# A hybrid decoder trunk: weight sums and low parts formed by adding DMAs

## The chip, the core and the metric

The kernel runs on one core of a Trainium2 chip. The metric is the device time in microseconds of one execution. Five engines work side by side, each through its own queue in order: TensorE (matmuls), VectorE, ScalarE, GpSimd and SyncE (SP), which here only issues DMAs. A DMA that adds to what its destination holds is issued by GpSimd (`G.dma_start(..., accum_op=ADD)`).

## The reference

Two layers of a decoder trunk on 512 tokens of width 1024. Each layer does four things, each after an RMSNorm and added to the residual x:

```python
x = x + 0.5 * swiglu_ffn(h, ffn1_w_gate[l], ffn1_w_up[l], ffn1_w_down[l])   # (silu(h Wg) * (h Wu)) Wd, 2816 wide
z = h @ w_in[l]                                  # S5 group (384) | pooling group (256) | conv group (2 x 384)
x = x + concat(S5(z), pool(z), conv(z)) @ w_out[l]
x = x + cross_attention(h, m, wq, wk, wv, wo)    # 4 heads into 256 memory tokens, m = RMSNorm(mem)
x = x + 0.5 * swiglu_ffn(h, ffn2_w_gate[l], ffn2_w_up[l], ffn2_w_down[l])
```

and a final RMSNorm. Everything is float32.

## The kernel before

All float32 products are made of three matmuls on a split into a high part (rounded to the type fp32r) and a low part (the value minus its high part): high x high, high x low, low x high (`mm3`, lines 307 to 309). So every weight that is loaded passes through a split: ScalarE copies it to the high part, and VectorE, or GpSimd where `eng` is G, subtracts to get the low part (`wload`, lines 294 to 301). Raw weights, high parts and low parts have three buffers each (tags raw, wh and wl of the pool wp).

The first feed-forward (ffn1 of layer 0) is a plain one. The other three (ffn2 of layer 0, ffn1 and ffn2 of layer 1) are "seven-product" feed-forwards (`ffn7`): gate and up are computed together by seven half-size products in place of eight, on combinations of the tokens' halves and of the weights' quarters. The hidden width of 2816 is cut into units of 512 columns (five of them, and one of 256). A unit has four weight quarters of two tiles each, (0,0) and (1,0) from the gate, (0,1) and (1,1) from the up matrix. Three steps make sums of weights from them, until now on VectorE:

- `mix1` (line 478): t1 = quarter (0,0) + quarter (0,1), four tiles of 128x512, kept in four buffers of a pool of their own;
- `mix2` (line 482): quarter (0,1) += quarter (1,1), then quarter (0,0) += the new (0,1), two instructions of 128x1024 each;
- `mix3` (line 482): quarter (1,0) += the new (0,0), two more.

The unit's products follow in the order 1 (raw (0,0)), 2 (raw (1,0)), 5 (t1), 6 (mixed (0,0)), 3 (raw (1,1)), 7 (mixed (0,1)), then the down projection of the unit before, then 4 (mixed (1,0)). A product's weights are split two steps ahead of it. In the first unit of a feed-forward t1 and the first sum are formed on GpSimd while the phase before ends (`PairNorm.take`, lines 221 and 223), and the second sum and `mix3` by `sum_` on VectorE.

The mixer runs the input projections, the S5 scan (on TensorE, VectorE, ScalarE and GpSimd in turn), the pooling and a 31-tap convolution on VectorE (line 1053), and fills TensorE meanwhile with the cross-attention's keys and values of the 256 memory tokens (`cross_kv`): eight key tiles of 512 KB (four heads, two halves `dh` of a head) and eight value tiles of 512 KB. The low parts of all of these are subtracted by GpSimd (line 300), which also does the scan's products (lines 992, 1002, 1020) and the norms' powers (line 191). VectorE's steps of the scan are lines 991 to 1003, 1016 and 1022.

The order of each engine's instructions is written out ahead of the run by the framework's planner: it simulates the engines with its own cost model and issues, by priority (the program's order, with the scan and the convolution's end raised), what is ready in that simulation.

Of the kernel before, what the change touches and what calls it, by code (L numbers as in the profile page):

```python
# [9 lines left out]
F32 = mybir.dt.float32  # L10
F32R = mybir.dt.float32r
AF = mybir.ActivationFunctionType
# [5 lines left out]
P = 128  # L18
# [26 lines left out]
def trunk_kernel(ctx: ExitStack, tc: tile.TileContext, io, out, phases=None):  # L45
    nc = tc.nc
    V, A, G, T = nc.vector, nc.scalar, nc.gpsimd, nc.tensor
    ADD, SUB, MUL = ALU.add, ALU.subtract, ALU.mult
# [5 lines left out]
    NK = D // P  # L54
# [35 lines left out]
    def vt(name, shape=(P, 512), dt=F32):  # L90
        return vp.tile(list(shape), dt, tag="V", name=name)
# [10 lines left out]
    def ct_(name, shape, dt=F32):  # L102
        return cp.tile(list(shape), dt, tag="C", name=name)

    def mm(name, shape=(P, 512)):
        return mmp.tile(list(shape), F32, tag="mm", name=name)
# [97 lines left out]
    HK = NK // 2  # L204
# [86 lines left out]
        return rb  # L291


    def wload(src, shape, name, eng=None):
        raw = wp.tile(list(shape), F32, tag="raw", name=f"wr_{name}")
        nc.sync.dma_start(out=raw, in_=src)
        h = wp.tile(list(shape), F32R, tag="wh", name=f"wh_{name}")
        A.activation(out=h, in_=raw, func=AF.Copy)  # L298
        lo = wp.tile(list(shape), F32R, tag="wl", name=f"wl_{name}")
        (eng or V).tensor_tensor(out=lo, in0=raw, in1=h.bitcast(F32), op=SUB)  # L300
        return h, lo

    def wcols(w, r0, nk, c0, name, eng=None):
        return wload(w[r0:r0 + nk * P, c0:c0 + P].rearrange("(k p) c -> p k c", p=P), (P, nk, P), name, eng)

    def mm3(ps, wh, wl, ah, al, first, last, skip=False):
        T.matmul(ps, lhsT=wh, rhs=ah, start=first, stop=False, skip_group_check=skip)  # L307
        T.matmul(ps, lhsT=wh, rhs=al, start=False, stop=False, skip_group_check=skip)  # L308
        T.matmul(ps, lhsT=wl, rhs=ah, start=False, stop=last, skip_group_check=skip)  # L309
# [25 lines left out]
    def rows_pass(dst, w, k0, acts, dh, name, first, last, eng=None, marks=None):  # L335

        n = len(acts)
        got = []
        for j in range(0, n, 2):
            m = min(2, n - j)  # L340
            h, lo = wload(w[(k0 + j) * P:(k0 + j + m) * P, dsl(dh)].rearrange("(k p) c -> p k c", p=P), (P, m, H2),
                          f"{name}_{dh}{j}", eng)
            got += [(h[:, i, :], lo[:, i, :]) for i in range(m)]
            with tc.issue_after(marks[j // 2]) if marks else nullcontext():
                for t, ps in dst:
                    for i in range(m):
                        ah, al = acts[j + i]
                        mm3(ps, ah[:, tsl(t)], al[:, tsl(t)], got[j + i][0], got[j + i][1], first and j + i == 0,
                            last and j + i == n - 1)
        return got  # L350
# [81 lines left out]
    def ffn7(which, l, norm, nxt):  # L432


        wg, wu, wd = (io[f"{which}_w_{n}"][l] for n in ("gate", "up", "down"))
# [27 lines left out]
        class Unit:  # L463
# [10 lines left out]
            def mix1(self):  # L474
                a, b = self.raw[0, 0], self.raw[0, 1]
                t1 = self.raw["t1"] = [vt(f"wt_{self.nm}{k}", (P, self.W)) for k in range(HK)]
                for k in range(HK):
                    V.tensor_tensor(out=t1[k], in0=a[k // 2][:, k % 2, :], in1=b[k // 2][:, k % 2, :], op=ADD)

            def sum_(self, to, other):  # L480
                for a, b in zip(self.raw[to], self.raw[other]):
                    V.tensor_tensor(out=a, in0=b, in1=a, op=ADD)  # L482

            def mix2(self):
                self.sum_((0, 1), (1, 1))
# [77 lines left out]
        for u, un in enumerate(us):  # L563
            b = len(steps)
# [314 lines left out]
    def mixer(l, norm, nxt):  # L879
# [87 lines left out]
        conv_in(2)  # L967

        kv = cross_kv(l, mg)


# [150 lines left out]
    def cross_kv(l, mg):  # L1122
        wk, wv = io["xattn_wk"][l], io["xattn_wv"][l]
        ks, vs = [], []
        for hd in range(NH):
            ps = mm(f"kps{l}_{hd}", (P, 2, M))
            for dh in range(2):
                c0 = hd * HD + dh * P
                h, lo = wcols(wk, 0, NK, c0, f"k{l}_{hd}{dh}", G)
                for k in range(NK):  # L1130
                    mm3(ps[:, dh, :], h[:, k, :], lo[:, k, :], mg[k][:, 0, :], mg[k][:, 1, :], k == 0, k == NK - 1)
            kt = ct_(f"kT{l}_{hd}", (P, 2, 2, M), F32R)
            A.activation(out=kt[:, 0], in_=ps, func=AF.Copy)
            V.tensor_tensor(out=kt[:, 1], in0=ps, in1=kt[:, 0].bitcast(F32), op=SUB)
            ks.append(kt)
        vs = [[ct_(f"v{'hl'[z]}{l}_{m}", (P, D), F32R) for z in range(2)] for m in range(NM)]
        for hf in range(2):
            pss = [mm(f"vps{l}_{hf}{m}") for m in range(NM)]
            for q in range(4):
                h, lo = wload(wv[q * 2 * P:(q + 1) * 2 * P, hf * 512:(hf + 1) * 512].rearrange("(k p) c -> p k c", p=P),  # L1140
                              (P, 2, 512), f"v{l}_{hf}{q}", G)
                for kk in range(2):
                    k = q * 2 + kk
                    for m in range(NM):
                        mh = mg[k][:, 0, m * P:(m + 1) * P]
                        ml = mg[k][:, 1, m * P:(m + 1) * P]
                        T.matmul(pss[m], lhsT=mh, rhs=h[:, kk, :], start=k == 0, stop=False)
                        T.matmul(pss[m], lhsT=mh, rhs=lo[:, kk, :], start=False, stop=False)
                        T.matmul(pss[m], lhsT=ml, rhs=h[:, kk, :], start=False, stop=k == NK - 1)
            for m in range(NM):  # L1150
                sl = slice(hf * 512, (hf + 1) * 512)
                A.activation(out=vs[m][0][:, sl], in_=pss[m], func=AF.Copy)
                V.tensor_tensor(out=vs[m][1][:, sl], in0=pss[m], in1=vs[m][0][:, sl].bitcast(F32), op=SUB)
        return ks, vs
# [222 lines left out]
```

## Time and profile before

| | |
|---|---|
| median of 3 runs | 2134.53 us (2134.12 to 2137.26) |
| profiled execution, its own time | 2135.13 us |
| its span | 2133.0 us |
| mean granted TensorE clock | 0.987 |
| TensorE busy | 2065.5 us (97%) |
| VectorE busy | 1551.3 us (73%) |
| ScalarE busy | 917.0 us (43%) |
| GpSimd busy | 356.8 us (17%) |
| DMA | 229.92 MB, mean 108 GB/s |

The span runs from the first to the last instruction of one execution. Matmuls overlap each other, so that a row's duration of 0.39 us is more than the distance between two starts. The granted clock is what TensorE was given, as a share of full speed. A row of a timeline has its start, its duration, engine, line, operation, output and inputs, shapes and count; in square brackets stands the idle time of the engine before it and what ended that. POOL is GpSimd, PE TensorE, DVE VectorE, ACT ScalarE.

### The profile page before, as it was taken

How to read it: one execution, taken by the hardware profiler on the slowest of the kernel's cores; microseconds unless marked ns; L12 is line 12 of the kernel's file. 1: busy time of each engine (PE TensorE's matmuls, PEld its weight loads, DVE VectorE, ACT ScalarE, POOL GpSimd, SP SyncE). 2: the span in 40 equal slices, each digit the busy share in tenths (PEclk: the TensorE clock that was granted, in tenths of full speed). 3: DMA queues.
4: the chain of work that ended last, by engine and by line, in shares of the span. 5: the costliest groups of instructions: out<-in, count | busy, mean ns of one | idle time of the engine just before them, and what ended most of it. 6: DMA issues, size and time to landing. Idle time of an engine off the chain costs nothing.

```text
span 2133.0 us, 27561 instructions
## 1 busy us (share of the span) xinstructions
PE 2065.5 (97%) x10228; PEld 1732.9 (81%) x10228; DVE 1551.3 (73%) x2574; ACT 917.0 (43%) x1528; POOL 356.8 (17%) x349
## 2 busy tenths in 40 slices
PE   7999999999999999999999999999999999999998
PEld 6778788888788878888878888888877887888886
DVE  5755677579855788787688877666996458887765
ACT  4423333334534464454445444444344345554443
POOL 0377000155400200000110000013661020000000
PEclk9999999998999999999999999999999999999999
DMA  5332445343421323332314223263443232332222
GB/s 170 101 104 82 117 150 165 108 137 107 125 88 60 119 80 119 119 119 79 119 40 147 83 88 108 80 217 97 122 134 109 70 134 79 119 107 91 74 60 84
DMA packets 226750, 229.92 MB, mean 108 GB/s; under 512 B 38478, under 2 KB 152888, under 8 KB 226616
## 3 DMA queue, kind: packets, MB, share of 16 engines
q1 hardware_dynamic: 225952, 227.10, 34.3%
q8 instruction: 80, 1.31, 0.3%
q10 hardware_dynamic: 664, 1.07, 0.1%
q14 instruction: 54, 0.44, 0.1%
HBM read 213.77 MB, written 12.58 MB: 106 GB/s over the span
## 4 chain that ended last, share of the span: by engine, by line
PE 83%; DVE 8%; DMA 3%; ACT 3%; issue 2%; POOL 1%; SPq 1%; DVEq 0%; POOLq 0%; ACTq 0%
PE pxffn L308 6%; PE pxffn L309 6%; PE pxffn L307 6%; PE pddffn L308 5%; PE pddffn L309 5%; PE pddffn L307 5%; PE pzffn L307 3%; PE pzffn L308 3%; PE pzffn L309 3%; PE pdffn L309 2%; PE pdffn L307 2%; PE pdffn L308 2%; DVE cacc L1053 1%; PE qps L308 1%; PE qps L309 1%
## 5 line engine op out<-in xcount | busy, mean ns | idle before, releaser
L308 PE MATMUL pddffn<-wl_dffn,hhffn 128*128 128x512 f32 x480 | 188.9, 394 | 0.0
L309 PE MATMUL pddffn<-wh_dffn,hlffn 128*128 128x512 f32 x480 | 188.1, 392 | 0.0
L307 PE MATMUL pddffn<-wh_dffn,hhffn 128*128 128x512 f32 x480 | 185.8, 391 | 0.0
L1053 DVE SCALAR_TENSOR_TENSOR cacc<-ch,convw,cacc 128x510 f32<-128x510 f32 (+28 forms) x174 | 127.8, 735 | 6.2 <-ACT cacc L1051 2.5
L374 DVE SCALAR_TENSOR_TENSOR x<-pddffn,x 128x512 f32<-128x512 f32 x120 | 82.2, 686 | 62.8 <-PE pddffn L309 62.8
L308 PEld LDWEIGHTS pddffn<-wl_dffn,hhffn 128*128 128x128 f32 x480 | 90.2, 188 | 18.2
L309 PEld LDWEIGHTS pddffn<-wh_dffn,hlffn 128*128 128x128 f32 x480 | 90.2, 188 | 18.0
L307 PEld LDWEIGHTS pddffn<-wh_dffn,hhffn 128*128 128x128 f32 x480 | 89.8, 188 | 18.3
L221 POOL TENSOR_TENSOR wt_first_ffn<-wr_first_ffn,wr_first_ffn 128x512 f32<-128x512 f32 x12 | 16.8, 1426 | 503.3 <-DMA wr_first_ffn<-in_ffn_w_up_dram 503.3
L482 DVE TENSOR_TENSOR wr_ffn<-wr_ffn,wr_ffn 128x1024 f32<-128x1024 f32 (+1 forms) x90 | 98.4, 1110 | 0.1
L300 POOL TENSOR_TENSOR wl_pl<-wr_pl,wh_pl 128x1024 fp32r<-128x1024 f32 x4 | 9.6, 2404 | 486.0 <-ACT wh_pl L298 486.0
L459 DVE TENSOR_TENSOR wl_dffn<-wr_dffn,wh_dffn 128x512 fp32r<-128x512 f32 x60 | 42.0, 705 | 39.7 <-PE pxffn L308 18.2
L535 ACT ACTIVATE hhffn<-htffn 128x512 fp32r<-128x512 f32 x60 | 35.6, 594 | 80.7 <-PE htffn L529 80.6
L307 PE MATMUL pgffn<-xh_ffn,wh_gffn 128*128 128x512 f32 x168 | 66.2, 394 | 0.0
L308 PE MATMUL pgffn<-xl_ffn,wh_gffn 128*128 128x512 f32 x168 | 66.0, 393 | 0.0
L309 PE MATMUL pgffn<-xh_ffn,wl_gffn 128*128 128x512 f32 x168 | 65.9, 392 | 0.0
L309 PE MATMUL puffn<-xh_ffn,wl_uffn 128*128 128x512 f32 x168 | 65.8, 392 | 0.0
L307 PE MATMUL puffn<-xh_ffn,wh_uffn 128*128 128x512 f32 x168 | 65.8, 392 | 0.0
L308 PE MATMUL puffn<-xl_ffn,wh_uffn 128*128 128x512 f32 x168 | 65.8, 392 | 0.0
L191 POOL TENSOR_TENSOR ss_final<-ss_final,nhalf 128x1 f32<-128x1 f32 x4 | 2.2, 550 | 350.2 <-DVE ss_final L190 350.2
L307 PE MATMUL pdffn<-wh_dffn,h_ffffn 128*128 128x512 f32 x144 | 57.9, 402 | 2.1 <-DVE sffn L394 2.1
L300 POOL TENSOR_TENSOR wl_v<-wr_v,wh_v 128x1024 fp32r<-128x1024 f32 x22 | 53.5, 2441 | 35.4 <-ACT wh_v L298 25.7
(745 smaller groups left out, 6735.7 us busy)
## 6 DMA issues: line engine op xcount, KB each, us to landing
wr_dffn<-in_ffn_w_down_dram SPq DMA_DIRECT2D x78, 512.0 KB
wr_ffn<-in_ffn_w_up_dram SPq DMA_DIRECT2D x48, 512.0 KB
wr_ffn<-in_ffn_w_gate_dram SPq DMA_DIRECT2D x48, 512.0 KB
wr_gffn<-in_ffn_w_gate_dram SPq DMA_DIRECT2D x21, 512.0 KB
wr_uffn<-in_ffn_w_up_dram SPq DMA_DIRECT2D x21, 512.0 KB
wr_k<-in_xattn_wk_dram SPq DMA_DIRECT2D x16, 512.0 KB
wr_v<-in_xattn_wv_dram SPq DMA_DIRECT2D x16, 512.0 KB
wr_q<-in_xattn_wq_dram SPq DMA_DIRECT2D x16, 512.0 KB
```

The costliest lines, as they stand in the source:

```text
L191: G.tensor_tensor(out=ss[:, 3:4], in0=ss[:, 2:3], in1=nhalf[:, 0:1], op=ALU.pow)
L221: G.tensor_tensor(out=t1[k], in0=a[k // 2][:, k % 2, :], in1=b[k // 2][:, k % 2, :], op=ADD)
L300: (eng or V).tensor_tensor(out=lo, in0=raw, in1=h.bitcast(F32), op=SUB)
L307: T.matmul(ps, lhsT=wh, rhs=ah, start=first, stop=False, skip_group_check=skip)
L308: T.matmul(ps, lhsT=wh, rhs=al, start=False, stop=False, skip_group_check=skip)
L309: T.matmul(ps, lhsT=wl, rhs=ah, start=False, stop=last, skip_group_check=skip)
L374: V.scalar_tensor_tensor(out=x_, in0=ps, scalar=scale, in1=x_, op0=MUL, op1=ADD)
L459: V.tensor_tensor(out=lo, in0=r, in1=h.bitcast(F32), op=SUB)
L482: V.tensor_tensor(out=a, in0=b, in1=a, op=ADD)
L535: A.activation(out=h, in_=pt, func=AF.Copy)
L1053: V.scalar_tensor_tensor(out=acc[:, d:], in0=h[:, 0:S - d], scalar=cw[:, TAPS - 1 - d:TAPS - d], in1=acc[:, d:], op0=MUL, op1=ADD)
```

## The change

The t1 sums of the units after the first are no longer computed from the loaded quarters: the gate's part is loaded a second time into t1 by SP, and the up matrix' part is added to it from HBM by an adding DMA. The in-place sums of all units become adding DMAs from SBUF to SBUF. In the mixers the low part of all value tiles, and of the key tiles with `dh` = 1, is made in two steps: ScalarE writes the negated high part (a rounded copy with scale -1), and an adding DMA adds the raw weight, from HBM for the values and from the raw tile for the keys. The subtractions of VectorE and GpSimd that did this go.

```diff
+    ADDING = "adding DMA"
+
     def wload(src, shape, name, eng=None):
         raw = wp.tile(list(shape), F32, tag="raw", name=f"wr_{name}")
         nc.sync.dma_start(out=raw, in_=src)
         h = wp.tile(list(shape), F32R, tag="wh", name=f"wh_{name}")
         A.activation(out=h, in_=raw, func=AF.Copy)
         lo = wp.tile(list(shape), F32R, tag="wl", name=f"wl_{name}")
-        (eng or V).tensor_tensor(out=lo, in0=raw, in1=h.bitcast(F32), op=SUB)
+        if eng is ADDING:
+
+            A.activation(out=lo, in_=raw, func=AF.Copy, scale=-1.0)
+            G.dma_start(out=lo, in_=raw if shape[1] > 2 else src, accum_op=ADD)
+        else:
+            (eng or V).tensor_tensor(out=lo, in0=raw, in1=h.bitcast(F32), op=SUB)
         return h, lo
...
                 for k in range(HK):
-                    V.tensor_tensor(out=t1[k], in0=a[k // 2][:, k % 2, :], in1=b[k // 2][:, k % 2, :], op=ADD)
+                    r0 = k * P
+                    nc.sync.dma_start(out=t1[k], in_=wg[r0:r0 + P, self.f0 * P:self.f0 * P + self.W])
+                for k in range(HK):
+                    r0 = k * P
+                    G.dma_start(out=t1[k], in_=wu[r0:r0 + P, self.f0 * P:self.f0 * P + self.W], accum_op=ADD)
 
             def sum_(self, to, other):
                 for a, b in zip(self.raw[to], self.raw[other]):
-                    V.tensor_tensor(out=a, in0=b, in1=a, op=ADD)
+                    G.dma_start(out=a, in_=b, accum_op=ADD)
...
-                h, lo = wcols(wk, 0, NK, c0, f"k{l}_{hd}{dh}", G)
+                h, lo = wcols(wk, 0, NK, c0, f"k{l}_{hd}{dh}", ADDING if dh else G)
...
-                              (P, 2, 512), f"v{l}_{hf}{q}", G)
+                              (P, 2, 512), f"v{l}_{hf}{q}", ADDING)
```

## Rows read from the trace of the kernel before

**Rows 1.** The page's busy times: share of the span, instructions.

```profile
PE 2065.5 (97%) x10228; PEld 1732.9 (81%) x10228; DVE 1551.3 (73%) x2574; ACT 917.0 (43%) x1528; POOL 356.8 (17%) x349
```

**Rows 2.** Busy time by stretch: engines, granted clock, DMA share, GB/s.

```profile
853.00:914.00 61.00, 61.00 (x278) 50.46 (x277) 45.54 (x62) 27.98 (x42) 0.00 (x0) 1.00 0.34 104
...
485.00:570.00 85.00, 80.33 (x444) 69.07 (x443) 80.05 (x111) 37.27 (x50) 49.96 (x24) 0.90 0.38 115
1518.00:1610.00 92.00, 84.97 (x499) 72.42 (x499) 83.71 (x124) 41.51 (x56) 57.27 (x27) 0.96 0.39 119
...
503.00:510.00 7.00, 7.00 (x35) 7.00 (x35) 6.93 (x12) 2.81 (x4) 4.42 (x4) 0.52 0.63 186
524.00:534.00 10.00, 10.00 (x42) 8.97 (x42) 9.15 (x13) 3.57 (x6) 3.58 (x2) 0.50 0.34 116
...
752.00:756.00 4.00, 3.43 (x10) 2.42 (x11) 4.00 (x7) 3.96 (x9) 0.00 (x0) 0.57 0.00 0
```

**Rows 3.** TensorE's waits: who for whom, us in total, times, longest.

```profile
PE yps L1007 <- DVE sy L1003: 5.9, 3, 3.1
PE pxffn L307 <- ACT xc_ffn L258: 5.5, 8, 1.3
...
PE xp_ffn L256 <- DVE xc_ffn L259: 3.9, 3, 1.4
PE gps L1032 <- DVE sys L1022: 3.2, 1, 3.2
...
PE yps L1006 <- DVE sy L991: 1.5, 1, 1.5
```

**Rows 4.** Groups by line: count, busy us, mean ns, idle before.

```profile
L482 DVE TENSOR_TENSOR wr_ffn<-wr_ffn,wr_ffn 128x1024 f32<-128x1024 f32 (+1 forms) x90 | 98.4, 1110 | 0.1
...
L300 POOL TENSOR_TENSOR wl_v<-wr_v,wh_v 128x1024 fp32r<-128x1024 f32 x22 | 53.5, 2441 | 35.4 <-ACT wh_v L298 25.7 <-PE kps L309 6.1 <-issue 3.0
...
L300 POOL TENSOR_TENSOR wl_k<-wr_k,wh_k 128x1024 fp32r<-128x1024 f32 x16 | 40.9, 2560 | 16.5 <-ACT wh_k L298 15.8 <-DVE sy L993 0.8
...
L478 DVE TENSOR_TENSOR wt_ffn<-wr_ffn,wr_ffn 128x512 f32<-128x512 f32 (+1 forms) x60 | 36.0, 634 | 9.4 <-DMA wr_ffn<-in_ffn_w_up_dram 9.3
```

**Rows 5.** Timelines of SP, VectorE and ScalarE before the unit at 910 us.

```profile
882.60 1.57 SPq L656 DMA_DIRECT2D wr_ffn<-in_ffn_w_up_dram  x2
...
896.83 2.35 DVE L482 TENSOR_TENSOR wr_ffn<-wr_ffn,wr_ffn 128x1024 f32<-128x1024 f32 x2
...
919.98 1.06 ACT L448 ACTIVATE wh_ffn_3p<-wr_ffn 128x1024 fp32r<-128x1024 f32 x1 [2.96 <-PE pyffn L309]
```

**Rows 6.** The page's DMA queue; two loads of 512 KB on the chain.

```profile
q1 hardware_dynamic: 225952, 227.10, 34.3%
...
700.22 4.21 DMA wr_xo<-in_xattn_wo_dram
...
1041.40 5.28 DMA wr_dffn<-in_ffn_w_down_dram
```

**Rows 7.** Timelines of VectorE and GpSimd at the second feed-forward's start.

```profile
738.10 1.21 DVE L482 TENSOR_TENSOR wr_first_ffn<-wr_first_ffn,wr_first_ffn 128x1024 f32<-128x1024 f32 x1
...
732.26 0.55 POOL L191 TENSOR_TENSOR ss_ffn<-ss_ffn,nhalf 128x1 f32<-128x1 f32 x1 [5.06 <-DVE ss_ffn L190]
741.31 1.46 POOL L191 TENSOR_TENSOR ss_ffn<-ss_ffn,nhalf 128x1 f32<-128x1 f32 x1 [8.49 <-DVE ss_ffn L190]
```

**Rows 8.** Timeline of VectorE: one scan step beside a subtraction, and alone.

```profile
474.94 2.86 DVE L993 TENSOR_TENSOR sy<-sy,ssw 128x512 f32<-128x512 f32 x1 [0.63 <-POOL ssw L992]
...
509.10 0.68 DVE L993 TENSOR_TENSOR sy<-sy,ssw 128x512 f32<-128x512 f32 x1
```

**Rows 9.** A value tile's copy; the value matmuls' first and last start, both mixers.

```profile
544.33 1.06 ACT L298 ACTIVATE wh_v<-wr_v 128x1024 fp32r<-128x1024 f32 x1 [1.65 <-PE vps L1149]
...
L1147 PE MATMUL vps<-wh_v,mg x32: 387/389/792, 538.6 to 564.1; 128*128 128x512 f32 x32
...
L1147 PE MATMUL vps<-wh_v,mg x32: 387/389/396, 1569.8 to 1597.9; 128*128 128x512 f32 x32
```

## The prediction

> **What bounds the kernel now.** I read the busy times first [rows 1]: TensorE is busy 97% of the span, VectorE 73%, GpSimd 17%. So work taken from VectorE or GpSimd is worth only what TensorE waits for. Then the busy time by stretch [rows 2]. In the steady part of a seven-product feed-forward, here 853 to 914 us, TensorE is busy for all 61.0 us at full clock, although VectorE works 45.5 us of them. In the two mixers' key and value stage it is not: 80.3 of 85 us in the first and 85.0 of 92 in the second, with VectorE at 80.1 and 83.7. Inside the first lie two stretches with the clock granted at its lower level, 1.2 instead of 2.4 GHz: 503 to 510 at 0.52 and 524 to 534 us at 0.50, which cost 3.4 + 5.0 = 8.4 us. The start of the second feed-forward has 4 us at 0.57, worth 1.7. Last, what TensorE waits for [rows 3]: in the mixers VectorE's steps of the S5 scan, 5.9 + 3.2 + 1.5 = 10.6 us; at the starts of the three seven-product feed-forwards evacuations of transposes, 5.5 + 3.9 = 9.4 us, about 3.1 each. What this change can win lies in these waits and the low clock behind them: about 19 us in the mixers and 4 to 5 at a feed-forward's start.
>
> **The feed-forwards' steady part.** VectorE loses the t1 sums and the in-place sums [rows 4]: 60 x 0.634 (36.0 us), 90 x 1.110 (98.4 us) and 12 more of the first units at about 1.1 (13 us), some 148 us. TensorE never waited there, so I count it at nothing. In exchange come, per full unit, four loads of 256 KB on SP's queue, four accumulates of 256 KB from HBM and six of 512 KB inside SBUF on GpSimd's queue, which is otherwise empty in these stretches. What hides them is the lead time [rows 5]: for the unit after the steady one the last up-weights are asked for at 882.6 to 884.2 us, land some 5 us later (5.28 for a load of this size [rows 6]), and the second pair of in-place sums ends at 899.2; the first product that reads it is split on ScalarE at 919.98. An accumulate's whole time, call it D, enters twice in that chain: 889 + D + 1 for the first pair, and the same again for the second. With D = 6 that is 903, with D = 14 it is 919: cover is gone only above about 14 us. The four t1 accumulates stand ahead in GpSimd's queue, but their loads wait only for tiles that the last unit gave back. Term: 0; if the cover fails, each of some 15 units pays the excess.
>
> The transfers' sum bounds this from the other side. The one queue moved 227.1 MB in 34.3% of 2133 us [rows 6], so 512 KB cost the 16 engines 1.69 us; the steady unit has a DMA share of 0.34, 20.7 us [rows 2]. Added: 1.05 MB of loads, 3.4 us, and 4.19 MB of accumulates, 13.5 us if they cost one pass, 40.6 us if three (two reads and a write, one after the other). The sum is 38 to 65 us of 61. I take two passes, 51 us: it fits.
>
> **The feed-forwards' starts.** In the two that follow attention the first unit's sums stand between the last tokens' residual and their normalisation [rows 7]: one of 1.21 us at 738.10, ahead of the mean square in VectorE's order, the other right after it, and beside that one GpSimd's power takes 1.46 us instead of 0.55. Gone, the chain is 1.2 + 0.9 = 2.1 us shorter; TensorE waits about 3.1 us behind it. I take 2.0 each, bounds +1 (an accumulate's issue stands before the power on GpSimd) and -4.8 (all waits and the low clock); the third start, after a feed-forward, had no sum in this place. Term: -4.
>
> **The mixers, GpSimd's side.** GpSimd's subtractions of 2.44 (values, 22 rows of which 16 are these) and 2.56 us (keys, 16) [rows 4] hold up VectorE: the same step of the scan takes 0.68 us alone and 2.86 beside one [rows 8]. I count 18 VectorE instructions stretched like this in the two stages, against the shortest of their kind: 17.6 us beside the keys' subtractions and 5.2 beside the values'. All the values' and half the keys' go: 5.2 + 8.8 = 14.0 us less on a VectorE that is busy 94% and 91% of these stretches, in the chain TensorE waits for. I let half of the 10.6 us of waits go, 5.3, and 3.7 of the 8.4 us of low clock. Term: -9; bounds 0 (the order fixed in TensorE's queue meets another late operand) and -19 (all of both).
>
> **The mixers, the low part's way.** It was ScalarE's copy, then GpSimd's 2.4 us; now two copies of 1.06 us [rows 9] and an accumulate, whose D no row of this trace shows. The nearest rows are loads of 512 KB: 4.21 and 5.28 us [rows 6]. One pass more for reading the destination gives 4.21 + 1.69 = 5.9, two passes 5.28 + 3.4 = 8.7; from below it is 4.2. I take 6. Each weight tile has three buffers, and in the value stage ScalarE's copy waits for TensorE to give one back [rows 9]. A tile's cycle is then two copies, D, and 12 matmuls at 61.0/278 = 0.219 us each [rows 2], 2.63; a third of it is one tile's pace: (2.12 + 6 + 2.63)/3 = 3.58 us. Eight tiles took 25.5 and 28.1 us to the start of the last three matmuls, 0.7 more to their end [rows 9]: 3.27 and 3.60 each. Lost: 8 x 0.31 + 0 = 2.5 us. Half the keys alternate with the old way, and their matmuls lie among the scan's, so D hides there. What queues behind a waiting accumulate is the scan's products on GpSimd, which stood behind waiting subtractions before; ScalarE gets 24 x 1.06 = 25 us more, in stretches in which it is busy 37 of 85 us. Term: +3; bounds 0 (D up to 5.0) and +17 (D = 8.7).
>
> The Trainium skill's DMA: Bandwidth & Descriptors (Anatomy of one DMA — SWDGE (gpsimd) path) fits a DMA issued by GpSimd as 2.0 us plus bytes at 436 GB/s, 3.2 us for 512 KB; by that estimate, which no run here shows and which is not said of accumulates, the last term is 0 and the time 2122.
>
> **Sum.** 0 - 4 - 9 + 3 = -10 us on the profiled execution's 2135.1 (span 2133.0): 2125.1. That execution stands 0.6 above the median of 2134.5, so 2125 stays.
>
> **Rivals.**
> 1. The waits vanish whole: with the scan on time no low clock follows, the value stage keeps its pace and the starts give 3 each: -6 - 14 = 2115, to a few us less. For it: the low stretches follow waits. Against it: VectorE stays busy with the convolutions.
> 2. The issue itself meets VectorE. GpSimd's power of 0.55 us took 1.46 beside a two-input sum [rows 7]; if each accumulate's issue waits like that for one such instruction of 1.2 us, D is 7.2, a tile's pace (2.12 + 7.2 + 2.63)/3 = 3.98, lost 8 x (7.97 - 6.87) = 8.8, and -13 + 8.8 = -4.2: 2131, no change. It is no change too where the saved VectorE time only moves slack. The Trainium skill's same page (SWDGE vs HWDGE vs iDMA) says that GpSimd writes its descriptors to rings in SBUF and that VectorE can lock it out meanwhile; the power's row agrees in kind, no row shows an issue.
> 3. Slower: the value stage becomes a ring of three late low parts. It decides from D = 8.8: pace 4.52, lost 8 x (9.03 - 6.87) = 17.3, more than the 13 won by 4.3 (0.2%). At D = 10 the pace is 4.92, lost 23.7: 2146. For it: 8.7 is one end of my bounds, and the values' source is HBM. Against it: TensorE has scan and gate matmuls to put between.
> 4. The DMA engines are full in the feed-forwards: at three passes 65 us of transfers per 61 us unit, 4 x 15 = 60 us less the 13 won: up to 2182. Against: the lead time, and that the last units are half as wide.
>
> **Chances.** Forecast (2121 to 2130) 0.42, rival 1 0.13, rival 2 0.20, rival 3 0.17, rival 4 0.08. A measurement of this kernel tells about 0.2% (4.3 us) from no change. Faster 0.55, within 0.2% 0.20, slower 0.25. The likeliest case's own range is 2121 to 2130; the range for 8 in 10 is 2114 to 2149, which leaves out rival 4 and the far end of rival 1.
>
> **What would show it.** VectorE's busy time down by about 160 us, GpSimd's by about 60 less what issues cost, TensorE's matmul count the same. The stretched scan steps back at 0.7 us beside the values; TensorE's waits for the scan below 6 us; the power at the two starts back at 0.55. The value stage's 25.5 and 28.1: up by 3 in sum is my D, up by 10 or more in sum is rival 3. No wait of TensorE or ScalarE on an accumulate in the steady feed-forward; any there is rival 4's side and makes the forecast wrong, as would scan waits as long as now.

## The result, and the profile after

The changed kernel takes 2172.84 us (median of 4 runs, 2170.38 to 2175.34) against 2134.36 (4 runs) for the kernel before: ratio 1.0174, 95% interval 1.0158 to 1.0189. It is slower by 38.5 us; 2125 was forecast, and 2149 was the upper end of the range.

From the first start of one phase's transposes on TensorE to the next one's, the first mixer went from 195.5 to 214.5 us and the second from 191.8 to 207.8: +19.0 and +16.0. All other phases together changed by +3.6, the start before them by 0.3. So the place is the mixers, and there the value stage. Page of the changed kernel: busy times, the two queues that carry nearly all bytes (packets, MB, share of 16 engines), and the group of the values' accumulates on GpSimd (busy, mean ns, idle before):

```profile
PE 2077.8 (96%) x10228; PEld 1739.9 (80%) x10228; DVE 1405.2 (65%) x2412; ACT 944.0 (43%) x1552; POOL 457.5 (21%) x511
...
q1 hardware_dynamic: 234592, 241.26, 35.4%
q0 software_dynamic: 28832, 75.51, 19.2%
...
L305 POOL DMA_DIRECT2D wl_v<-in_xattn_wv_dram x16 | 19.5, 1220 | 83.6 <-issue 43.9 <-ACT wh_v L300 14.9 <-ACT su L1046 10.6
```

Against [rows 1] VectorE has lost 146 us (160 were forecast), and GpSimd, whose busy time now holds the issues, has gained 101. The last row is the trace of what went wrong: before 16 issues GpSimd sat idle 83.6 us, over half of it for "issue", which is a wait for nothing that the profile shows. What TensorE waits for in the changed kernel (us, times, longest):

```profile
PE vps L1159 <- DMA wl_v<-in_xattn_wv_dram: 35.1, 12, 5.5
...
PE pxffn L314 <- ACT xc_ffn L258: 4.2, 6, 1.4
PE kps L316 <- DMA wl_k<-wr_k: 3.4, 2, 2.9
PE xp_ffn L256 <- DVE xc_ffn L259: 3.2, 3, 1.2
...
PE yps L1018 <- DVE sy L1014: 1.8, 2, 1.4
```

Beside [rows 3] the scan's waits of 10.6 us are down to 1.8, but a new wait of 35.1 us for the values' low parts has come. The value matmuls of the changed kernel, first to last start, in both mixers:

```profile
L1158 PE MATMUL vps<-wh_v,mg x32: 387/393/632, 530.2 to 584.0; 128*128 128x512 f32 x32
...
L1158 PE MATMUL vps<-wh_v,mg x32: 388/389/796, 1583.7 to 1634.5; 128*128 128x512 f32 x32
```

The changed kernel's busy time in these stretches and in the steady feed-forward, columns as in [rows 2]:

```profile
530.20:584.00 53.80, 35.62 (x107) 24.69 (x106) 26.39 (x34) 21.16 (x25) 14.66 (x10) 0.81 0.74 165
1583.70:1634.50 50.80, 33.77 (x111) 22.49 (x110) 29.71 (x35) 21.13 (x25) 14.54 (x10) 0.90 0.76 164
...
851.00:912.00 61.00, 61.00 (x278) 50.49 (x277) 38.26 (x54) 27.88 (x41) 8.79 (x10) 1.00 0.73 188
```

Eight value tiles take 53.8 and 50.8 us where they took 25.5 and 28.1 [rows 9]. TensorE works 66% of that time, and its clock is granted at 0.81 and 0.90. The steady feed-forward is as full as before: 61.0 of 61.0 us, with the DMA share up from 0.34 to 0.73.

GpSimd's timeline in the first value stage of the changed kernel says what the low parts wait for (start, duration; idle time before in brackets):

```profile
523.66 1.25 POOL L305 DMA_DIRECT2D wl_v<-in_xattn_wv_dram  x1 [1.92 <-ACT wl_v L304]
530.65 1.23 POOL L305 DMA_DIRECT2D wl_v<-in_xattn_wv_dram  x1 [5.74 <-PE kps L316]
538.37 1.21 POOL L305 DMA_DIRECT2D wl_v<-in_xattn_wv_dram  x1 [6.49 <-issue]
547.01 1.21 POOL L305 DMA_DIRECT2D wl_v<-in_xattn_wv_dram  x1 [7.43 <-issue]
...
560.59 1.23 POOL L305 DMA_DIRECT2D wl_v<-in_xattn_wv_dram  x1 [5.92 <-issue]
```

ScalarE's timeline there has two of the negated copies:

```profile
532.99 1.99 ACT L304 ACTIVATE wl_v<-wr_v 128x1024 fp32r<-128x1024 f32 x2
```

They were ready at 534 and 535 us; their accumulates were issued at 538.37 and 547.01. All issues lie 6.5 to 9.6 us apart, and the median from issue to landing is 6.4. The chain of the changed kernel has two of these accumulates, from issue to landing:

```profile
530.65 7.38 DMA wl_v<-in_xattn_wv_dram
...
553.47 6.80 DMA wl_v<-in_xattn_wv_dram
```

They land at 538.03 and 560.27, and the next ones are issued at 538.37 and 560.59. In both mixers each of the 14 issues that follow another comes 0.32 to 0.34 us after the landing of the one before: one value accumulate is on its way at a time. Landing times in the changed kernel (KB each, median us):

```profile
wr_ffn<-wr_ffn POOLq DMA_DIRECT2D x72, 512.0 KB, 4.8
...
wt_ffn<-in_ffn_w_up_dram POOLq DMA_DIRECT2D x48, 256.0 KB, 5.8
...
wl_v<-in_xattn_wv_dram POOLq DMA_DIRECT2D x16, 512.0 KB, 6.4
```

GpSimd's timeline of the changed kernel in a feed-forward, with the issues of four t1 sums:

```profile
876.24 2.69 POOL L489 DMA_DIRECT2D wt_ffn<-in_ffn_w_up_dram  x3 [7.75 <-DMA wt_ffn<-in_ffn_w_gate_dram]
881.17 0.86 POOL L489 DMA_DIRECT2D wt_ffn<-in_ffn_w_up_dram  x1 [2.24 <-DVE wl_ffn_2p L466]
```

Three t1 sums go out within 2.7 us, the fourth about 5 us after the first, when that one has landed; in 14 of the 15 units the fourth comes 0.3 us after that landing. The difference is in the pieces. A t1 sum or a key tile has one piece per partition; a value tile from HBM has two. The packets of this queue show it. In the run with the values alone (below) it carries their 16 accumulates, 272 packets each:

```profile
q0 software_dynamic: 4352, 8.39, 2.5%
```

In the run with the keys alone it carries eight of the same size, 144 packets each:

```profile
q0 software_dynamic: 1152, 4.19, 1.0%
```

My theory from here: GpSimd's descriptors lie in a ring of limited memory (`dynamic_dma_scratch_size=1024` where the kernel is built) that holds three DMAs of 128 pieces and only one of 256, and the next issue waits for it to empty.

### The profile page after: what moved, and what is told of

It is laid out like the page before. It is cut to its first block, busy times and chain, and to the rows that moved or that the text cites. A ratio compares the mean times of both kernels' runs of the same rounds, so it can differ in the third digit from the quotient of the medians.

```text
span 2171.9 us, 28147 instructions
## 1 busy us (share of the span) xinstructions
PE 2077.8 (96%) x10228; PEld 1739.9 (80%) x10228; DVE 1405.2 (65%) x2412; ACT 944.0 (43%) x1552; POOL 457.5 (21%) x511
## 4 chain that ended last, share of the span: by engine, by line
PE 83%; DVE 6%; issue 4%; DMA 3%; ACT 2%; POOL 1%; SPq 0%; POOLq 0%; DVEq 0%; ACTq 0%
PE pxffn L316 5%; PE pxffn L315 5%; PE pxffn L314 5%; PE pddffn L315 5%; PE pddffn L316 5%; PE pddffn L314 5%; PE pzffn L314 3%; PE pzffn L315 3%; PE pzffn L316 3%; PE pgffn L315 2%; PE pgffn L314 2%; PE pgffn L316 2%; PE puffn L316 2%; PE puffn L314 2%; PE puffn L315 2%
## 5 line engine op out<-in xcount | busy, mean ns | idle before, releaser
L493 POOL DMA_DIRECT2D wr_ffn<-wr_ffn x90 | 78.5, 887 | 583.6 <-DVE x L381 241.7
L489 POOL DMA_DIRECT2D wt_ffn<-in_ffn_w_up_dram x60 | 53.2, 1025 | 154.8 <-DMA wt_ffn<-in_ffn_w_gate_dram 76.5
L546 ACT ACTIVATE hhffn<-htffn 128x512 fp32r<-128x512 f32 x60 | 35.8, 596 | 105.7 <-PE htffn L540 105.7
L466 DVE TENSOR_TENSOR wl_dffn<-wr_dffn,wh_dffn 128x512 fp32r<-128x512 f32 x60 | 41.2, 686 | 45.4 <-PE pxffn L315 21.5
L1159 PE MATMUL vps<-wl_v,mg 128*128 128x512 f32 x64 | 31.9, 498 | 35.2 <-DMA wl_v<-in_xattn_wv_dram 35.1
L547 DVE TENSOR_TENSOR hlffn<-htffn,hhffn 128x512 fp32r<-128x512 f32 x60 | 41.2, 687 | 32.7 <-ACT hhffn L546 32.7
L315 PE MATMUL qps<-xl_att,wh_q 128*128 128x256 f32 (+1 forms) x176 | 60.9, 346 | 0.0
```

Of the source, the lines that this page charges most:

```text
L466: V.tensor_tensor(out=lo, in0=r, in1=h.bitcast(F32), op=SUB)
L489: G.dma_start(out=t1[k], in_=wu[r0:r0 + P, self.f0 * P:self.f0 * P + self.W], accum_op=ADD)
L493: G.dma_start(out=a, in_=b, accum_op=ADD)
L546: A.activation(out=h, in_=pt, func=AF.Copy)
L547: V.tensor_tensor(out=lo, in0=pt, in1=h.bitcast(F32), op=SUB)
```

## Experiments

Each kernel is compared with the kernel before on the same chip. The first four tell the values from the rest, and the ring from the three weight buffers.

**The values alone.** The kernel before, with only this of the change:

```diff
-                              (P, 2, 512), f"v{l}_{hf}{q}", G)
+                              (P, 2, 512), f"v{l}_{hf}{q}", ADDING)
```

> The kernel before with only the value tiles' low parts by adding DMAs. Theory (the value stage alone): 2165 to 2178, value stage 50 to 55 us in each mixer, issues of the values' DMAs 6 to 9 us apart. Rival (it takes the feed-forwards' traffic or the keys' DMAs too): below 2155.

2182.71 us, ratio 1.0215 (1.0183 to 1.0246). TensorE waits 32.3 us for wl_v, and the issues are 6.5 to 9.3 us apart. The time lies above the 2165 to 2178 that were expected, and the value stages, 47.1 and 56.6 us, on either side of their 50 to 55. The whole loss is here, and more: the rest of the change gives some 9 us back.

**All but the values.** The changed kernel with `G` again in that line.

> The changed kernel with the value tiles' low parts subtracted by GpSimd again; sums in the feed-forwards and half the keys stay adding DMAs. Theory (the value stage alone costs the time): the wait of the value matmuls for their low parts (35 us) is gone, the value stage is back at 26 to 29 us, and the time is 2125 to 2138. Rival (the adding DMAs of the feed-forwards cost too, through traffic or the order): above 2145.

2129.54 us, ratio 0.996 (0.9943 to 0.9976): faster than before. The mixers take 189.9 and 188.4 us, 5.6 and 3.4 less than before: 9.0, which is the size forecast for them.

**Twice the descriptor memory.** Two small tiles are trimmed to make room.

```diff
-    nc = _bacc.Bacc("TRN2", target_bir_lowering=False, num_devices=1, dynamic_dma_scratch_size=1024)
+    nc = _bacc.Bacc("TRN2", target_bir_lowering=False, num_devices=1, dynamic_dma_scratch_size=2048)
```

> The changed kernel with GpSimd's DMA scratch of 2048 instead of 1024 bytes (two small tiles have fewer buffers to make room). Theory (the ring of descriptors holds one value DMA of 256 pieces at a time): three can be on their way, their issues come 3 to 5 us apart, the idle time of GpSimd that no wait explains goes from 44 us to under 10, and the time is 2133 to 2150. Rival (three buffers per weight tile and a long way of the low part set the pace whatever the ring): issues stay 6 to 9 us apart, 2168 to 2176.

2149.04 us, ratio 1.0053 (1.0035 to 1.0072): 1.2 of the 1.74% is gone, with no instruction of the change touched. On every engine the order of the instructions is that of the changed kernel too, here and in the run with 1536 bytes below, so the planner has no part in this. The waits for wl_v fall from 35.1 to 16.0 us, although one accumulate now takes 7.8 us instead of 6.4, with up to three on their way. GpSimd's idle time before these issues, 43.9 us of it for "issue" in the changed kernel, has none of that left (expected: under 10); it now waits for ScalarE's copies:

```profile
L305 POOL DMA_DIRECT2D wl_v<-in_xattn_wv_dram x16 | 19.9, 1242 | 47.9 <-ACT wl_v L304 39.2 <-DMA wl_v<-in_xattn_wv_dram 8.7
```

**The values' raw tile as source,** which gives pieces of 4096 bytes, one per partition:

```diff
-            G.dma_start(out=lo, in_=raw if shape[1] > 2 else src, accum_op=ADD)
+            G.dma_start(out=lo, in_=raw, accum_op=ADD)
```

> The changed kernel with the values' DMAs adding from the raw tile in SBUF (128 pieces of 4096 bytes) instead of from HBM (256 of 2048). Theory (the ring counts pieces): half the pieces, three on their way in the same ring, issues 3 to 5 us apart, 2133 to 2150; the raw tile is held until the DMA lands, which may cost a few us of later loads. Rival (buffers): 2168 to 2176 or more, since the raw tile comes free later.

2146.78 us, ratio 1.0042 (1.0026 to 1.0058). The memory is as small as in the changed kernel; half as many pieces do the same as twice the memory. The source's place changes here too, and slightly the order of instructions in the mixers, but both stay in the run above. What both have in common is more accumulates in flight.

**1536 bytes,** all else as in the changed kernel.

> The changed kernel with the memory for GpSimd's DMA descriptors at 1536 instead of 1024 bytes. Theory: 1024 hold three DMAs of 128 pieces and one of 256 (so one of 256 takes between a half and two thirds of them), and 1536 should hold two of the values' DMAs: issues go in pairs, and the time comes near that with 2048 bytes, 2147 to 2157 us, value stages 42 to 48 us. Rival (the time goes with the bytes, not with whole DMAs): the middle between 2172.8 and 2149.0, about 2161 us. If 1536 still held one, the time would stay at 2173.

2144.56 us, ratio 1.0035 (1.0021 to 1.0048): no worse than 2048, and better than the 2147 to 2157 expected. In this run's GpSimd timeline two issues stand 2.1 us apart, so two accumulates are on their way:

```profile
542.54 1.19 POOL L305 DMA_DIRECT2D wl_v<-in_xattn_wv_dram  x1
544.62 1.21 POOL L305 DMA_DIRECT2D wl_v<-in_xattn_wv_dram  x1 [0.90 <-ACT wl_v L304]
550.41 1.22 POOL L305 DMA_DIRECT2D wl_v<-in_xattn_wv_dram  x1 [4.58 <-ACT su L1046]
```

There are never more than two. And the four t1 sums of a feed-forward's unit, which went out as three and one, now go out together:

```profile
797.92 3.58 POOL L489 DMA_DIRECT2D wt_ffn<-in_ffn_w_up_dram  x4 [6.54 <-DMA wt_ffn<-in_ffn_w_gate_dram]
```

One size fits all of this. The most packets of this queue ever on their way are 432 in the changed kernel (three times 144), 576 here (four times 144) and 816 with 2048 bytes (three times 272). If 1024 bytes have room for 432 to 543 packets (an estimate: three times 144 go, twice 272 don't), half as much again, 648 to 815, holds two value accumulates and not three, and twice as much holds three. The step goes with whole DMAs: one to two gives all there is. So the ring explains some 30 us, from 1.0174 to 1.0035. But 16 us stay between this run and the one without the values (0.996), enough to keep it slower than the kernel before. The next runs ask for those.

**Every second value tile.**

```diff
-                              (P, 2, 512), f"v{l}_{hf}{q}", ADDING)
+                              (P, 2, 512), f"v{l}_{hf}{q}", ADDING if q % 2 else G)
```

> The changed kernel with only every second value tile (odd q) made by an adding DMA; the others are subtracted on GpSimd as before. Theory (GpSimd's ring takes one value DMA at a time, and the three weight buffers bound what is left): two accumulates now stand at least two tiles apart, some 6.6 us, about as long as one takes (6.4 us), so neither binds: 2126 to 2136 us, value stages 26 to 33 us each, TensorE's waits for wl_v below 6 us in the two mixers together. Rival (each value tile that goes by an accumulate costs by itself, 43 us over 16 tiles, 2.7 us each): half of the way from 2129.5 to 2172.8, 2151 us.

2130.69 us, ratio 0.9978 (0.9967 to 0.9989). The values' cost is not so much a tile: against the run without them eight accumulates cost 0.2%, 4 us (the intervals overlap), and the next eight 2.0%, 42 us. TensorE's waits for wl_v, 9.6 us, are above the bound of 6, and the value stages, 33.3 and 33.6 us, just above 33. The ring still binds here, which the theory denied: five of the six issues that follow another come 0.32 to 0.34 us after its landing, with 8.1 us from issue to landing. Half the tiles just leave TensorE little to wait for.

**Four weight buffers,** paid for by four general buffers; first the control that only takes those four away (both at 1536 bytes).

```diff
-    bp = ctx.enter_context(tc.tile_pool(name="bp", bufs=20))
+    bp = ctx.enter_context(tc.tile_pool(name="bp", bufs=16))
...
-        h = wp.tile(list(shape), F32R, tag="wh", name=f"wh_{name}")
+        h = wp.tile(list(shape), F32R, tag="wh", bufs=4, name=f"wh_{name}")
...
-        lo = wp.tile(list(shape), F32R, tag="wl", name=f"wl_{name}")
+        lo = wp.tile(list(shape), F32R, tag="wl", bufs=4, name=f"wl_{name}")
...
```

> The changed kernel with 1536 bytes for descriptors and with 16 instead of 20 general buffers (pool bp); three buffers per weight tag as before. It is the control for the run with four. Theory and rival alike: if the four buffers taken away are not missed, as with 1536 bytes alone, 2141 to 2152 us, value stages 38 to 42 us.

> The control with four instead of three buffers for the high and the low parts of the weights (16 general buffers pay for them). Theory (a weight tile's cycle of two copies, an accumulate of 7.8 us and its matmuls is shared by three buffers): with four the pace goes from (2.12 + 7.8 + 2.63)/3 = 4.2 to /4 = 3.1 us a tile, which is no more than the 3.3 of before: value stages 28 to 34 us, 10 to 17 us less than the control, 2128 to 2138 us. Rival (the scan and the values hold each other up in the in-order queues of ScalarE, GpSimd and SP, whatever the buffers): within 4 us of the control.

The control alone takes 2172.97 us, ratio 1.017 (1.0149 to 1.0192): that expectation was wrong. The general buffers are missed, or the planner's other order costs; the run doesn't part the two. With four weight buffers 2173.91, 1.0172 (1.0154 to 1.019). The value stages, 36.3 and 38.9 us against the control's 41.2 and 36.6, don't shorten in sum by more than 2.6 us. My cycle of three buffers forecast 10 to 17; it finds no support, though the comparison is blurred by what the control lost and by the order of instructions, which differs between the two on every engine.

**Half of the value loads.**

```diff
-    def wload(src, shape, name, eng=None):
-        raw = wp.tile(list(shape), F32, tag="raw", name=f"wr_{name}")
-        nc.sync.dma_start(out=raw, in_=src)
+    def wload(src, shape, name, eng=None, again=False):
+        if not again:
+            kept_raw[0] = wp.tile(list(shape), F32, tag="raw", name=f"wr_{name}")
+            nc.sync.dma_start(out=kept_raw[0], in_=src)
+        raw = kept_raw[0]
...
+                              (P, 2, 512), f"v{l}_{hf}{q}", ADDING, again=q % 2 == 1)
```

> The changed kernel with 1536 bytes for descriptors, and of the raw value tiles only every second one is loaded: the next one's high part and negated copy are made from the same raw tile (that part of the values is left out), while all 16 accumulates stay, each from its own place in HBM. Theory (with the ring widened the 16 DMA engines are full in the value stage: a tile's load takes 1.69 us of them and its accumulate 3.4, worked out from 2.5% of the span for 16 of them in the run with the values alone; 8 x 5.1 = 41 us a mixer): four loads less take 6.8 us a mixer, value stages 30 to 34 us instead of 40 and 38, 2127 to 2137 us. Rival (the time that an accumulate takes from issue to landing, or the in-order queues, set the pace and not the sum of bytes): value stages 37 us or more, 2140 to 2150 us, as with all the loads.

2137.33 us, ratio 1.0001 (0.9988 to 1.0014): 0.34%, 7 us, below the run with all loads, half of what full DMA engines would give and more than the rival allows. The value stages, 37.1 and 35.8 us, are near the rival's; but the profiled execution took 2143.57 us, well above the median, so its stages show little of the 7 us. Busy time of the value stages in the run at 1536 bytes with all loads (DMA share in the second to last column):

```profile
527.60:567.50 39.90, 31.35 (x107) 21.27 (x106) 24.68 (x36) 21.21 (x25) 12.30 (x9) 0.91 0.92 203
1564.70:1602.40 37.70, 31.01 (x111) 21.32 (x110) 24.80 (x34) 20.43 (x24) 11.74 (x9) 0.94 0.96 232
```

The run with half the loads:

```profile
528.70:565.80 37.10, 30.41 (x106) 21.86 (x105) 24.98 (x33) 19.30 (x24) 11.23 (x8) 0.86 0.90 178
1563.20:1599.00 35.80, 31.07 (x112) 21.16 (x111) 24.79 (x34) 20.43 (x24) 11.66 (x9) 0.95 0.87 178
```

The run without the values:

```profile
530.30:558.20 27.90, 25.69 (x105) 19.25 (x104) 24.54 (x33) 13.74 (x17) 19.18 (x8) 1.00 0.39 133
1560.00:1590.30 30.30, 27.87 (x106) 20.04 (x105) 26.01 (x33) 12.30 (x15) 18.05 (x8) 0.94 0.38 121
```

With the ring widened the DMA engines are busy 92% and 96% of the value stage. With half the loads they still are 90% and 87%: SP, with fewer loads ahead, issues those of the output projection earlier (in the first mixer from 537.5 us on, with all the loads from 545.2). The run was meant to empty the engines and didn't.

**Keys alone, feed-forwards alone.** The kernel before with only the one or the other part of the change.

> The kernel before with only the keys' half (dh = 1) made by adding DMAs; the feed-forwards' sums and the values as before. Theory: the gain that is left without the values comes from here, since GpSimd's subtractions no longer stretch VectorE's scan steps: 2126 to 2132 us (3 to 8 us below before), mixers shorter by 2 to 6 us each, feed-forwards within 1 us. Rival (the gain comes from the feed-forwards' starts): 2134 to 2138 us here.

> The kernel before with only the feed-forwards' sums made by loads and adding DMAs; keys and values as before. Theory: nothing, since TensorE never waited for these sums in the steady part and the starts showed no gain: 2133 to 2139 us, within 0.2% of before. Rival (my forecast's term for the starts): 4 us less, about 2131 to 2133, and the first GpSimd power at the two starts back at 0.55 us.

Keys alone: 2127.02 us, ratio 0.9963 (0.9949 to 0.9976). Feed-forwards alone: 2133.97, ratio 0.9986 (0.9973 to 0.9999). Most of the gain is the keys'; the feed-forwards give 0.2 to 5.8 us, an interval that holds next to nothing as well as the forecast's 4. The rival's sign is not there: GpSimd's power at the two starts takes 0.90 and 0.87 us, not 0.55. The keys' profile (of the slowest of its seven executions, 2133.33 us) does not show the gain where it was put: it keeps 8.2 us of scan waits (5.3 for sy, 2.9 for the gates), and of its mixers only the second is shorter, 187.0 us against 191.8.

**All keys,** values on GpSimd, looking for a faster version.

```diff
-                h, lo = wcols(wk, 0, NK, c0, f"k{l}_{hd}{dh}", ADDING if dh else G)
+                h, lo = wcols(wk, 0, NK, c0, f"k{l}_{hd}{dh}", ADDING)
```

> The changed kernel with the values subtracted on GpSimd as before and all eight key tiles, not half of them, made by adding DMAs. Theory (what this change wins is VectorE's relief from GpSimd's subtractions, which a key's accumulate gives while there is time to hide it): the other half of the keys gives as much again at best, 2122 to 2130 us. Rival (two accumulates of keys in a row come late for TensorE, as the values' did): waits of kps for wl_k above 8 us and 2131 to 2140 us.

2139.12 us, ratio 1.0013 (0.9999 to 1.0028). The rival's time, but not its reason: kps waits 5.8 us for wl_k, not over 8, and the scan's gates wait 6.8 us for VectorE. The other half of the keys loses what the first half won. Below the kernel before, by less than half a per cent each, lie the runs without the values and with the keys alone (both 0.996), with half the values (0.9978) and with the feed-forwards alone (0.9986).

## Why the prediction was wrong

**The step that failed: the mixers' low part's way.** The forecast costed a value tile as (2.12 + D + 2.63)/3, a pace for three tiles on their way at once. The price D = 6 was right for one accumulate (6.4 measured). What the sum took for granted is that GpSimd can issue the next accumulate while one is in flight. With 256 pieces each and 1024 bytes of descriptor memory it can't; tiles go out 6.5 to 9.6 us apart instead of 3.58, and 16 of them cost 2.1% (1.0174 against 0.996), some 45 us, where the term said +3. Some 30 of these are the descriptor memory's, shown by the run at 1536 bytes. Rival 3 had the place, the wait and the sign (the two value stages are longer by 51 us in sum, over its 10), but the ring that it meant is that of the three weight buffers, and its condition, D above 8.8, was not what decided: at D = 6.4 a single one in flight is slower than three at D = 10. The trace of before showed no adding DMA, and its three weight buffers were in plain sight; the descriptor memory stands in the last lines of the same kernel and was not read against the number of pieces.

Rival 2 is not seen: the 16 issues take 1.19 to 1.25 us each, so none is stretched beside VectorE. Rival 1 fails with its condition: the value stage does not keep its pace.

The Trainium skill's DMA: Bandwidth & Descriptors (Anatomy of one DMA — SWDGE (gpsimd) path) gives, by its fit for a plain DMA, an estimate of 3.2 us for 512 KB; this trace has 4.8 from SBUF and 6.4 from HBM, and the measurement decides. The same page of the Trainium skill (SWDGE vs HWDGE vs iDMA) has the descriptors in rings in SBUF; the two runs with more descriptor memory fit that, and show that room in them can run out.

**The feed-forwards' steady part: right.** No TensorE wait on a sum there, 61.0 of 61.0 us busy, DMA share 0.73, 44.5 us of transfers where two passes had given 51. Rival 4 is out.

**The starts: not won in the profile.** VectorE's timeline at the second feed-forward's start, before:

```profile
737.50 0.68 DVE L372 TENSOR_TENSOR x<-pwo,x 128x512 f32<-128x512 f32 x1
...
741.03 0.20 DVE L190 TENSOR_SCALAR ss_ffn<-ss_ffn 128x1 f32<-128x1 f32 x1
...
742.81 1.41 DVE L234 SCALAR_TENSOR_TENSOR xn_ffn<-x,ss_ffn,gb_ffn 128x512 f32<-128x512 f32 x2 [0.45 <-POOL ss_ffn L191]
```

And in the changed kernel:

```profile
757.32 0.68 DVE L379 TENSOR_TENSOR x<-pwo,x 128x512 f32<-128x512 f32 x1
...
759.72 0.20 DVE L190 TENSOR_SCALAR ss_ffn<-ss_ffn 128x1 f32<-128x1 f32 x1
762.54 1.42 DVE L234 SCALAR_TENSOR_TENSOR xn_ffn<-x,ss_ffn,gb_ffn 128x512 f32<-128x512 f32 x2 [2.62 <-POOL ss_ffn L191]
```

Its GpSimd timeline there:

```profile
761.06 0.87 POOL L493 DMA_DIRECT2D wr_first_ffn<-wr_first_ffn  x1 [4.19 <-issue]
761.62 0.89 POOL L191 TENSOR_TENSOR ss_ffn<-ss_ffn,nhalf 128x1 f32<-128x1 f32 x1
```

The mean square comes 2.40 us after the residual's start, where before it came at 741.03, 3.53 after the one at 737.50: the 1.2 us of the VectorE sum are won, as forecast. Then the power, ready at 759.9, stands in GpSimd's queue behind an accumulate whose issue waits until 761.06, 0.65 us after the accumulate before it has landed, and starts at 761.62. Residual to normalisation takes 5.22 us, before 5.31 (to 742.81). The start of the last feed-forward is alike: the power is ready at 1811.3 and starts at 1813.68. What was named for the bound of +1, an issue ahead of the power, took back what was won, so that the -2.0 each is not there.

**VectorE's relief in the mixers: right in size, its way only in part.** VectorE's busy time in the two mixers falls from 310.4 to 296.9 us, by 13.5 where 14.0 were forecast. In the run without the values the two mixers are 9.0 us shorter, the term's -9. But that run's scan waits are

```profile
PE gps L1043 <- DVE sys L1033: 4.6, 2, 2.4
...
PE yps L1018 <- DVE sy L1014: 1.9, 2, 1.4
```

6.5 us, not below the 6 that were to show it: the waits gave 4.1 where 5.3 were forecast. More came from the clock, granted at 0.98 and 0.97 in these mixers and at 0.96 in both before: about 6 us, an estimate from clock times length, where 3.7 were forecast out of the first mixer's 8.4; both mixers together lose some 15 by their 0.96. That the sum came out has luck in it: this run keeps GpSimd's subtractions of the values, whose 5.2 us of relief the term had counted in, and its order of instructions is another one. The 1.8 us of the changed kernel are no sign either way, since TensorE itself is late there.

**What stays open.** With the ring widened the values still cost 16 us. Three things hold there together: DMA engines busy over 90%, an accumulate of 7.8 us with two on their way, and in-order queues in which ScalarE's copies stand behind steps of the scan and the scan's product behind issues. Four buffers did not clearly shorten the stage, half the loads gave back 7 us without emptying the engines; which of the three sets the pace is not shown.

## What to carry to other kernels

Before a stage is given to DMAs that GpSimd issues, count how many of them its descriptor memory holds at once: pieces times DMAs in flight, not bytes. A transfer's own time is no pace; the pace is that time divided by the number on its way. Here the descriptor memory set that number, one where the three buffers allowed more; whether the buffers would set it next is not shown. And what is queued on the issuing engine behind an issue that waits, here a norm's power, waits with it.

## What was not expected of the hardware

- 1024 bytes of descriptor memory let three DMAs of 128 pieces go, but one of 256; with 1536 four of 128 went, and two of 256. The issue that found no room started 0.3 us after the landing that made it.
- An issue costs GpSimd some 0.9 us for 128 pieces (2.69 for three t1 sums) and 1.22 for 256.
- An accumulate from HBM takes twice a load's share of the DMA engines: 2.5% of a span of 2180.7 us for 16 of them in the run with the values alone, 3.4 us each, where a load of this size takes 1.69 [rows 6].
